# Eighteen of 22 up-projection pairs by Strassen products, and a down stage of its own, in a one-core decoder step

## The chip, the core and the metric

The kernel runs as one program on 1 core of a Trainium2 chip. The metric is the device time of one execution in microseconds (us); of several executions the median is given. The core has five engines: TensorE (PE, matmuls, with weight loads beside them), VectorE (DVE), ScalarE (ACT), GpSimd (POOL) and SyncE (SP), which issues nearly all DMA transfers. Each engine runs its instructions in the order in which the program issued them and waits at an instruction until its operands are there.

## What is computed

One layer of a decoder in float32, for 1,024 prompt tokens and 8 sequences of 4 sample tokens, 1,056 columns in all. The change lies in its last part, the feed-forward network (FFN):

```python
# D_MODEL = 1024, D_FF = 2816
merged = sigmoid(g_M) * (hm @ w_branch_m) + sigmoid(g_A) * (ha @ w_branch_a)
x  = LN1(ALPHA * x + gate1 * (merged @ w_out))
h2 = LN0(x) * (1 + scale2) + shift2
u  = h2 @ w_up + b_up                        # (tokens, 2 * D_FF)
u' = conv_b + sum_j ux[:, j:j+L] * conv_w[j] # causal depthwise convolution, width 3
f  = (gelu(u'_a) * u'_g) @ w_down + b_down   # a: first half of u', g: second half
x  = LN2(ALPHA * x + gate2 * f)
```

In the convolution a prompt token sees the two tokens before it; a sample sequence has two history columns of its own. The last two columns of u of every sequence are outputs too.

## The kernel before, in words

**Numbers and tiles.** Every float32 operand is split into a high part (a cast) and a low part (value minus high part), and each product is three matmuls: high by high, high by low, low by high. Activations lie with features on the 128 partitions and the 1,056 tokens along the free axis, and one such tile of 128 x 1056 float32 (528 KB) fills a slot of a pool of 43 (`slot`, L124; `drop` gives it back). Tokens are worked in three tiles of 384, 384 and 288. `Stream` (L385) carries the weights of direct blocks: `load` issues the DMA of a raw weight part, `prep` makes its high part on ACT (L422) and its low part on DVE (L426), `ahead_of` keeps the next part split and the one after on its way. `group` (L440) makes one output block of 128 rows for one token tile: 8 parts of the contraction by 3 matmuls. Its result lies in one of three PSUM banks used in turn (`lbank`, L146).

**Side work.** The program is one function. Work that is not matmuls is written as generators in a queue, `sides`. `pulse(us)` (L167), called beside each matmul group, advances a planner's clock; for every planned microsecond it takes `rate[0]` steps of the generator at the head (`step_side`, L159). So the rates decide where in each engine's order the side work lands. `later(us, fn)` (L156) puts off one action, mostly a store.

**Strassen pairs.** Ten pairs of blocks of the input projection are made in another way, by the class `Pair` (L1388) and the loop `fast` (L1491). Two output blocks, 1,024 inputs and 1,056 tokens are cut in halves, and seven products of half size (24 matmuls of 264 columns for each of two halves of the tokens) take the place of eight. `tprep` (L1341) makes sums and differences of the activations once; `Pair.step` 0 to 4 makes those of each pair's weights and splits them; `product` (L1451) runs the matmuls in a ring of eight PSUM banks (L1385) and evicts: product 1 by a copy on ACT, products 6, 7 and 5 by an add on DVE (L1465 to L1475), and the results by `put` (L1479), an add of bank, bias and a running sum.

**The FFN before.** The up projection makes 44 direct blocks; block j of the first half and block 22+j of the second form chunk j. ACT evicts u with its bias (L1869, sample tokens apart at L1871). The generator `post` (L1895) does the convolution on DVE, one TENSOR_SCALAR (L1877) and two SCALAR_TENSOR_TENSOR (L1882) over the prompt and three small steps for the samples (L1889 to L1891); then gelu on ACT (L1904) for a first-half block, or the gating multiply (L1908) and the split into `ahi` and `alo` (L337, L338) for a second-half block. Nothing of it leaves the chip's own memory. The down projection is worked in groups of three chunks that are run between up blocks as soon as their chunks are made (`down_group`, L2017): the first group is evicted by ACT into eight accumulators `facc` (L2036), later ones are added by DVE (L2038). After the sixth group `pre` (L1963) scales `facc` by the gate on ACT (L1966), transposes it 128 tokens at a time (PE, banks PD) and adds x1 (L1985), while the last up blocks run. The last group, of four chunks, is made with tokens as output rows (`product`, L2152), and its loop gates, adds, and makes LN2; the last chunk's convolution is done in pieces between (`post_now`).

## Time and profile before

| | |
|---|---|
| median of 3 runs | 1998.91 us (1998.17 to 1999.92) |
| profiled execution, its own time | 1998.65 us |
| its span in the trace | 1996.7 us |
| mean granted TensorE clock | 0.992 |
| matmuls and transposes | 12,837, 1933.1 us busy |
| DVE / ACT / POOL busy | 1114.6 / 737.1 / 301.4 us |
| DMA | 216.03 MB, mean 108 GB/s |

Times in rows of the trace count from the start of the span. In the timeline the first number is an instruction's start, the second its duration, and brackets hold how long its engine stood idle before it and what ended that. Rows of groups give busy time and the mean in ns of one instruction, and behind the second bar the idle time before them. In the table of windows each row is a stretch of time: its length, then the busy time (and count) of PE, weight loads, DVE, ACT and POOL, then granted clock, DMA share and GB/s. The FFN's direct blocks of the whole width begin at about 1245 us of the span, the last stage at about 1930.

### The profile page before, as it was taken

Reading aid. Unit: us, or ns where it says so; the run is one execution under the profiler, and the core shown is the slowest. Engines: PE = TensorE matmul, PEld = TensorE weight load, DVE = VectorE, ACT = ScalarE, POOL = GpSimd, SP = SyncE. Lnnn points to the kernel's source line nnn. Section 1 sums busy time; section 2 is a strip of 40 time slices with the busy share of each in tenths; the row PEclk is TensorE's granted clock in tenths of the full one; section 3 lists DMA queues with packets and bytes.
Section 4 is the critical chain, followed back from the end, with each engine's and each line's share of the span. In section 5 each row is a group of like instructions: output and inputs, shape, how many; then the busy total and the mean of one; then the engine's idle time right before and its main releaser. Section 6 shows DMA issues by size and latency. Waiting matters only on the chain. (4 is left out here: it accounts for less than half of the span.)

```text
span 1996.7 us, 32196 instructions
## 1 busy us (share of the span) xinstructions
PE 1933.1 (97%) x12837; PEld 1834.7 (92%) x12837; DVE 1114.6 (56%) x2374; ACT 737.1 (37%) x1530; POOL 301.4 (15%) x592
## 2 busy tenths in 40 slices
PE   6999999999999999999999999999999999999996
PEld 4999998988899889898889999999999999999995
DVE  5676665556655455563533455574454464546579
ACT  4431234444444554643312355343131312222331
POOL 2000000433441321212000333100000000000007
PEclk9999999999999999999999999999999999999998
DMA  9224342564434103343985141111212020111533
GB/s 296 88 88 157 97 119 79 150 177 134 99 103 127 66 22 121 110 136 107 348 282 166 62 127 55 48 37 46 61 34 62 27 69 27 49 47 48 193 130 129
DMA packets 222942, 216.03 MB, mean 108 GB/s; under 512 B 9745, under 2 KB 199873, under 8 KB 222761
## 3 DMA queue, kind: packets, MB, share of 16 engines
q1 hardware_dynamic: 222013, 213.38, 35.0%
q8 instruction: 100, 1.64, 0.3%
q10 hardware_dynamic: 780, 0.61, 0.1%
q14 instruction: 49, 0.40, 0.1%
HBM read 164.12 MB, written 51.87 MB: 108 GB/s over the span
## 5 line engine op out<-in xcount | busy, mean ns | idle before, releaser
L448 PE MATMUL L<-mhi,whi 128*128 128x384 f32 (+1 forms) x1248 | 408.0, 327 | 4.8 <-DVE r L1824 3.0
L448 PE MATMUL L<-mhi,wlo 128*128 128x384 f32 (+1 forms) x1248 | 403.8, 324 | 1.1 <-DVE wlo L426 1.1
L448 PE MATMUL L<-mlo,whi 128*128 128x384 f32 (+1 forms) x1248 | 404.1, 324 | 0.1
L448 PE MATMUL L<-hhi,whi 128*128 128x384 f32 (+1 forms) x1120 | 370.9, 331 | 0.2
L448 PE MATMUL L<-hlo,whi 128*128 128x384 f32 (+1 forms) x1120 | 362.1, 323 | 0.1
L448 PE MATMUL L<-hhi,wlo 128*128 128x384 f32 (+1 forms) x1120 | 361.7, 323 | 0.0
L426 DVE TENSOR_TENSOR wlo<-wraw,whi 128x1024 fp32r<-128x1024 f32 (+1 forms) x128 | 150.2, 1174 | 305.5 <-ACT whi L422 305.4
L448 PEld LDWEIGHTS L<-mhi,whi 128*128 128x128 f32 x1248 | 235.4, 189 | 6.7 <-DVE r L1824 3.2
L448 PEld LDWEIGHTS L<-mhi,wlo 128*128 128x128 f32 x1248 | 235.1, 188 | 1.7 <-DVE wlo L426 1.7
L448 PEld LDWEIGHTS L<-mlo,whi 128*128 128x128 f32 x1248 | 235.4, 189 | 0.3 <-DVE mlo L1797 0.3
L448 PEld LDWEIGHTS L<-hhi,whi 128*128 128x128 f32 x1120 | 211.2, 189 | 6.9 <-issue 4.8
L448 PEld LDWEIGHTS L<-hlo,whi 128*128 128x128 f32 x1120 | 211.5, 189 | 0.7 <-DVE hlo L1325 0.3
L1869 ACT ACTIVATE u<-L,vT 128x384 f32<-128x384 f32 (+1 forms) x132 | 71.7, 544 | 380.0 <-PE L L448 379.9
L448 PEld LDWEIGHTS L<-hhi,wlo 128*128 128x128 f32 x1120 | 211.1, 188 | 0.0
L422 ACT CAST whi<-wraw 128x1024 fp32r<-128x1024 f32 (+1 forms) x128 | 128.4, 1005 | 32.9 <-DMA wraw<-in_w_up 21.8
L448 PE MATMUL L<-ahi,whi 128*128 128x384 f32 (+1 forms) x432 | 139.7, 323 | 0.0
L448 PE MATMUL L<-ahi,wlo 128*128 128x384 f32 (+1 forms) x432 | 139.5, 323 | 0.0
L448 PE MATMUL L<-alo,whi 128*128 128x384 f32 (+1 forms) x432 | 139.4, 323 | 0.0
L1882 DVE SCALAR_TENSOR_TENSOR y<-u,vT,y 128x1023 f32<-128x1023 f32 (+3 forms) x92 | 113.7, 1236 | 2.5
L1892 POOL COPY ucol<-u 128x2 f32<-128x2 f32 x44 | 10.3, 234 | 631.4 <-ACT u L1869 631.4
L2038 DVE TENSOR_TENSOR facc<-L,facc 128x384 f32<-128x384 f32 (+1 forms) x120 | 62.7, 523 | 58.1 <-PE L L448 58.0
L448 PEld LDWEIGHTS L<-alo,whi 128*128 128x128 f32 x432 | 81.2, 188 | 0.0
(579 smaller groups left out, 3574.8 us busy)
## 6 DMA issues: line engine op xcount, KB each, us to landing
wada<-in_w_ada SPq DMA_DIRECT2D x44, 512.0 KB
wraw<-in_w_up SPq DMA_DIRECT2D x44, 512.0 KB
wraw<-in_w_in SPq DMA_DIRECT2D x32, 512.0 KB
fraw<-in_w_in SPq DMA_DIRECT2D x20, 512.0 KB
wraw<-in_w_down SPq DMA_DIRECT2D x24, 384.0 KB
vD<-fdst SPq DMA_DIRECT2D x8, 528.0 KB
ogD<-fdst SPq DMA_DIRECT2D x8, 528.0 KB
v<-vD SPq DMA_DIRECT2D x8, 528.0 KB
```

The lines of the kernel that those rows point to most:

```text
L422: A.copy(hi[:, :n], t[:, :n])
L426: V.tensor_tensor(lo[:, :n], t[:, :n], hi[:, :n].bitcast(F32), op=OP.subtract)
L448: T.matmul(ps[:, :nt], x[:, c], y[:, t0:t0 + nt], start=i == 0, stop=i == last)
L1869: A.activation(u[:, t0:t0 + n], ps[:, :n], AF.Identity, bias=b)
L1882: V.scalar_tensor_tensor(y[:, f:b], u[:, f - d:b - d], w[i], y[:, f:b], op0=OP.mult, op1=OP.add)
L1892: G.tensor_copy(aux["ucol"][:, c, 0:2], u[:, SEQ - 2:SEQ])
L2038: V.tensor_tensor(fx, ps[:, :nt], fx, op=OP.add)
```

## The change

Four chunks (0 to 3) keep their direct up blocks. The 18 pairs of chunks 4 to 21 go through `fast` as Strassen pairs, with results summed in place in their destination tiles (`inplace`). `first_up_pair`, 23 steps of side work during the last three direct blocks, joins h2's parts again and makes the sums of activations and of the first pair's weights. A convolution's first pass is now ACT's. Every u leaves for DRAM in some form: of the direct chunks u itself (`uD`); of chunks 4 to 10 the finished product of gelu and gate (`aD3`); of chunks 11 to 21 the second block convolved (`yD`) and the first block's u (`uD`).

The down projection then stands alone, in six groups of 3, 4, 4, 4, 3 and 4 chunks: [4, 5, 6], [7, 11, 12, 0], [8, 13, 14, 1], [9, 15, 16, 2], [10, 17, 3], [18, 19, 20, 21]. The generator `chunk` brings each chunk back, does what is left of it and splits it; `operands` takes side steps until a group's chunks are all issued. The fifth group goes through its output blocks once for each token tile (`down_by_tokens`), scales each by the gate and leaves transposes and the add of x1 as delayed steps, so that three of the nine fall behind the group. The rows for the last stage's gate come earlier (`gate_rows2`); `post_now` goes away. The diff, cut to its core:

```diff
+RATE_T, RATE_U, RATE_D, RATE_P = 0.75, 0.7, 0.8, 0.9
-    KG = [3, 3, 3, 3, 3, 3, 4]
+    ND = 4
+    WHOLE = 7
+    ready_, rest = deque(range(ND, ND + WHOLE)), deque(range(ND + WHOLE, 22))
+    KG = [3, 4, 4, 4, 3, 4]
+    chunks_of = [[ready_.popleft() for _ in range(3)]]
+    for i in range(4):
+        chunks_of.append([ready_.popleft(), rest.popleft()] + ([rest.popleft()] if i < 3 else []) + [i])
+    chunks_of.append(list(rest))
...
-    def tprep():
+    def tprep(joined=False):
         for kp in range(4):
+            if joined:
+                for k in (2 * kp, 2 * kp + 1):
+                    hf[k] = slot(name="hf")
+                    hi, lo = opnd["x"][k]
+                    V.tensor_tensor(hf[k], hi.bitcast(F32), lo.bitcast(F32), op=OP.add)
+                yield
...
-            u1, u2, u3, u5 = (u[:, g, :] for u in (U1, U2, U3, U5))
+            if self.inplace:
+                if p in (1, 6) and not g:
+                    self.dst[p // 6] = slot(name="fdst")
+                o = [quarters(self.dst[i])[:, g] if i in self.dst else None for i in range(2)]
...
-            for pos, p in enumerate((1, 3, 6, 2, 7, 4, 5) if n else (1, 3, 2, 6, 7, 4, 5)):
+            for pos, p in enumerate((1, 3, 2, 6, *order_) if not n and swap else (1, 3, 6, 2, *order_)):
...
+    def conv(c, u, y):
...
+        A.activation(y[:, :SEQ], u[:, :SEQ], AF.Identity, bias=b, scale=w[2])
+        A.copy(us[:, :, 2:6], to3(u[:, SEQ:]))
         G.tensor_copy(us[:, :, 0:2], aux["hist"][:, :, :, c])
+        yield
+        V.scalar_tensor_tensor(y[:, 1:SEQ], u[:, :SEQ - 1], w[1], y[:, 1:SEQ], op0=OP.mult, op1=OP.add)
+        yield
+        V.scalar_tensor_tensor(y[:, 2:SEQ], u[:, :SEQ - 2], w[0], y[:, 2:SEQ], op0=OP.mult, op1=OP.add)
+        yield
...
+    def post(c, u):
         y = slot(name="y")
+        yield from conv(c, u, y)
+        drop(u)
+        yield
+        if c >= 22:
+            if c - 22 < ND + WHOLE:
+                ya[c - 22] = y
+            else:
+                to_dram(yD, c, y)
+            return
+        A.activation(y, y, AF.Gelu_apprx_tanh)
+        yield
+        V.tensor_tensor(y, y, ya[c], op=OP.mult)
+        drop(ya.pop(c))
+        to_dram(aD3, c, y)
+        yield
...
+    def chunk(j):
...
+        if j in aD3:
+            y = load(aD3[j])
...
+        else:
+            u = load(uD[j])
+            if 22 + j in yD:
+                y2 = load(yD[22 + j])
...
+            else:
+                u2 = load(uD[22 + j])
...
+                yield from conv(22 + j, u2, y2)
...
+            yield from conv(j, u, y)
...
+            A.activation(y, y, AF.Gelu_apprx_tanh)
+            yield
+            V.tensor_tensor(y, y, y2, op=OP.mult)
+            drop(y2)
+        hi, lo = slot(F32R, "ahi"), slot(F32R, "alo")
+        A.copy(hi, y)
+        yield
+        V.tensor_tensor(lo, y, hi.bitcast(F32), op=OP.subtract)
...
+    def operands(gi):
+        base = sum(KG[:gi])
+        while len(acts2) < base + KG[gi]:
+            step_side()
+        return {k: acts2[base + k] for k in range(KG[gi])}
...
+    def down_by_tokens(gi):
+        a = operands(gi)
+        for ti in range(3):
+            for q in range(4):
...
+                for sub in range(2):
+                    down_block(gi, q, sub, ti, a)
+                    j = 2 * q + sub
+                    f = facc[j][:, t0:t0 + np_]
+                    A.activation(f, f, AF.Copy, scale=modT[:, 5, j, 0:1])
...
+            spread(pre(ti), 1.1)
...
+    def first_up_pair():
+        sums = tprep(True)
+        for i in range(23):
+            if i in (10, 11, 22):
+                upairs[0].step((10, 11, 22).index(i))
+            else:
+                next(sums)
+            yield
...
+    sides.append(first_up_pair())
+    rate[0] = RATE_T
+    for i in range(NF, 2 * ND):
+        if i == NF + 1:
+            upairs[0].load()
...
+    rate[0] = RATE_U
+    chunk_gens = deque(chunk(j) for j in dorder)
...
+    fast(upairs, up_end, (7, 5, 4), lambda n: None)
...
+    for _ in range(3):
+        chunk_gens.popleft()
+    for i in range(11):
+        sides.append(chunk_gens.popleft())
+    sides.append(gate_rows2())
+    sides.extend(chunk_gens)
+    for gi in range(len(KG) - 2):
+        rate[0] = RATE_D
+        down_group(gi)
+    rate[0] = RATE_P
+    down_by_tokens(len(KG) - 2)
```

Line numbers in the following rows are each program's own. The first place is DVE in the up projection. Before, in a direct chunk's second block (`wlo` is a weight's low part, `y` the convolution, `us` the sample columns, `alo` the low part for the down projection):

```order
L426 TENSOR_TENSOR wlo_834_15246<-wraw_830_15154,whi_833_15245 128x1024
L1877 TENSOR_SCALAR y_836_15263<-u_832_15182,vT_88 128x1024
L1882 SCALAR_TENSOR_TENSOR y_836_15263<-u_832_15182,vT_88,y_836_15263 128x1023
L1882 SCALAR_TENSOR_TENSOR y_836_15263<-u_832_15182,vT_88,y_836_15263 128x1022
L1889 TENSOR_SCALAR y_836_15263<-us_15183,vT_88 128x32
L1890 SCALAR_TENSOR_TENSOR y_836_15263<-us_15183,vT_88,y_836_15263 128x32
L1891 SCALAR_TENSOR_TENSOR y_836_15263<-us_15183,vT_88,y_836_15263 128x32
L1908 TENSOR_TENSOR y_831_15171<-y_831_15171,y_836_15263 128x1056
```

And in the change, in an early pair, where `fdst` is a pair's result (L1497 is `put`), and `flo` and `fq` are low parts of the next product's weights:

```order
L1497 SCALAR_TENSOR_TENSOR fdst_734_13349<-L0_71,vT_88,fdst_734_13349 128x264
L1907 SCALAR_TENSOR_TENSOR y_741_13507<-fdst_734_13349,vT_88,y_741_13507 128x1023
L1428 TENSOR_TENSOR flo_744_13529<-fsum_737_13430,fhi_743_13528 128x1024
L1909 SCALAR_TENSOR_TENSOR y_741_13507<-fdst_734_13349,vT_88,y_741_13507 128x1022
L1497 SCALAR_TENSOR_TENSOR fdst_727_13273<-PF_77,vT_88,fdst_727_13273 128x264
L1912 TENSOR_SCALAR y_741_13507<-us_13508,vT_88 128x32
L1913 SCALAR_TENSOR_TENSOR y_741_13507<-us_13508,vT_88,y_741_13507 128x32
L1914 SCALAR_TENSOR_TENSOR y_741_13507<-us_13508,vT_88,y_741_13507 128x32
L1497 SCALAR_TENSOR_TENSOR fdst_727_13273<-PG_78,vT_88,fdst_727_13273 128x264
L1448 TENSOR_TENSOR fq_745_13564<-fraw_736_13366,fq_745_13564 128x512
L1428 TENSOR_TENSOR flo_747_13568<-fsum_738_13431,fhi_746_13567 128x1024
```

A block's convolution steps stand directly behind its last `put`, and ahead of low parts of weights.

The second place is ACT at the end of the first down group. Before:

```order
L2036 ACTIVATE facc_737_13533<-L2_73,vT_88 128x384
L2036 ACTIVATE facc_737_13533<-L0_71,vT_88 128x384
L2036 ACTIVATE facc_737_13533<-L1_72,vT_88 128x288
L422 CAST whi_740_13568<-wraw_735_13492 128x1024
L1869 ACTIVATE u_743_13598<-L2_73,vT_88 128x384
```

In the change (L2101 is the eviction, `ld` a reloaded block; L1903 a convolution's first pass, L1904 its sample copy, L1995 the gelu, L2000 the cast that makes the operand):

```order
L2101 ACTIVATE facc_1011_17557<-L2_73,vT_88 128x384
L2101 ACTIVATE facc_1011_17557<-L0_71,vT_88 128x384
L2101 ACTIVATE facc_1011_17557<-L1_72,vT_88 128x288
L1903 ACTIVATE y_1014_17593<-ld_1013_17577,vT_88 128x1024
L1904 COPY us_17594<-ld_1013_17577 128x8x4
L1903 ACTIVATE y_1015_17605<-ld_1012_17575,vT_88 128x1024
L1904 COPY us_17606<-ld_1012_17575 128x8x4
L1995 ACTIVATE y_1015_17605<-y_1015_17605 128x1056
L2000 CAST ahi_1016_17619<-y_1015_17605 128x1056
```

Both passes, the gelu and the cast of chunk 0 stand behind the group's last eviction; `ahi_1016` is an operand of the second group, which follows on PE with no other work between.

The third place is DVE at the end of the third down group, in the change (L2103 adds into `facc`, L1997 multiplies by the gate, L2002 makes the low part):

```order
L2103 TENSOR_TENSOR facc_1011_17557<-L1_72,facc_1011_17557 128x288
L1907 SCALAR_TENSOR_TENSOR y_1080_18493<-ld_1077_18421,vT_88,y_1080_18493 128x1023
L1909 SCALAR_TENSOR_TENSOR y_1080_18493<-ld_1077_18421,vT_88,y_1080_18493 128x1022
L1912 TENSOR_SCALAR y_1080_18493<-us_18494,vT_88 128x32
L1913 SCALAR_TENSOR_TENSOR y_1080_18493<-us_18494,vT_88,y_1080_18493 128x32
L1914 SCALAR_TENSOR_TENSOR y_1080_18493<-us_18494,vT_88,y_1080_18493 128x32
L1997 TENSOR_TENSOR y_1080_18493<-y_1080_18493,y_1079_18445 128x1056
L2002 TENSOR_TENSOR alo_1082_18508<-y_1080_18493,ahi_1081_18507 128x1056
```

Here one convolution, the multiply and the low part of chunk 2, an operand of the fourth group, stand behind the third group's last add.

## The prediction

> **What bounds the kernel now.** I read the page's busy shares first, then the chain of waits, then the places that the change replaces.

> ```profile
> PE 1933.1 (97%) x12837; PEld 1834.7 (92%) x12837; DVE 1114.6 (56%) x2374; ACT 737.1 (37%) x1530; POOL 301.4 (15%) x592
> ```

> ```profile
> 1262.98 601.22 PE L L448 x3735
> ...
> 1868.33 0.87 PE PD L197 x8
> ```

> TensorE (PE) sets the pace of both FFN stages: in the chain (second fence) it runs 601 us on end, nothing waits in it. So the question is what the change saves on PE, and where VectorE (DVE) or ScalarE (ACT) becomes late. In the timeline, ACT's second eviction of one up block and of the next give the price of a direct block; ACT's first copy of one Strassen pair and of the next give that of a pair in the input projection.

> ```profile
> 1302.70 0.58 ACT L1869 ACTIVATE u<-L,vT 128x384 f32<-128x384 f32 x1 [2.75 <-PE L L448]
> ...
> 1314.26 0.58 ACT L1869 ACTIVATE u<-L,vT 128x384 f32<-128x384 f32 x1 [3.55 <-PE L L448]
> ```

> ```profile
> 183.09 0.38 ACT L1461 COPY hf<-L 128x264 f32<-128x264 f32 x1 [9.33 <-PE L L1457]
> ...
> 203.66 0.38 ACT L1461 COPY hf<-PE 128x264 f32<-128x264 f32 x1 [9.13 <-PE PE L1457]
> ```

> A direct block is 11.56 us (72 matmuls), a pair of blocks 23.12; a Strassen pair is 20.57 us (168 matmuls of 264 columns), so a product (24 matmuls) is 1.47.

> **What the change takes off PE.** 18 pairs x (23.12 - 20.57) = **45.9 us**. Also, three of the nine groups of transposes of the accumulated output (0.87 us each, the row at 1868.33) go behind the first products of the last stage, which DVE paces: **2.6**. In that stage the last block's convolution goes away, but those three tiles' adds come in.

> ```profile
> 1938.70:1960.00 21.30, 21.30 (x97) 17.35 (x96) 20.09 (x34) 5.03 (x7) 12.25 (x17) 1.00 0.21 69
> 1960.00:1980.60 20.60, 20.60 (x91) 14.86 (x90) 20.22 (x27) 4.98 (x4) 18.89 (x17) 1.00 0.44 159
> ```

> ```profile
> 1941.42 0.36 DVE L1877 TENSOR_SCALAR y<-u,vT 128x256 f32<-128x256 f32 x1
> ...
> 1945.19 0.69 DVE L2169 TENSOR_TENSOR L<-L,gp 128x512 f32<-128x512 f32 x1
> ```

> DVE (fourth number) is full; 3.8 us of it leave (1941.42 to 1945.19), and the third product, from which DVE paces, comes 2.6 later: **1.2** won. Gains 49.7 us.

> **What it adds: DVE in the early pairs.** In the input projection a pair leaves DVE 40% idle:

> ```profile
> 180.00:200.00 20.00, 20.00 (x166) 19.92 (x165) 11.87 (x22) 4.22 (x6) 0.00 (x0) 1.00 0.48 159
> ```

> ```profile
> L1416 DVE TENSOR_TENSOR flo<-fsum,fhi 128x1024 fp32r<-128x1024 f32 x20 | 24.5, 1224 | 17.4 <-ACT fhi L1415 17.1
> L1479 DVE SCALAR_TENSOR_TENSOR fdst<-L,vT,hf 128x264 f32<-128x264 f32 x28 | 13.5, 489 | 8.2 <-PE L L1457 8.1
> ...
> L1436 DVE TENSOR_TENSOR fq<-fraw,fq 128x512 fp32r<-128x512 f32 x10 | 6.8, 684 | 0.0
> ...
> L1411 DVE TENSOR_TENSOR fsum<-fraw 128x512 f32<-128x512 f32 x9 | 6.2, 687 | 1.4 <-DMA fraw<-in_w_in 1.3
> ...
> L1467 DVE TENSOR_TENSOR hf<-L,hf 128x264 f32<-128x264 f32 x9 | 3.9, 432 | 7.6 <-PE L L1457 7.6
> ```

> Here the pair also carries the convolution. Groups of DVE and then of ACT from 1245 to 1930 us:

> ```profile
> L1882 DVE SCALAR_TENSOR_TENSOR y<-u,vT,y 128x1023 f32<-128x1023 f32 x43 | 55.1, 1282 | 1.1
> ...
> L426 DVE TENSOR_TENSOR wlo<-wraw,whi 128x1024 fp32r<-128x1024 f32 x43 | 52.5, 1223 | 178.3 <-ACT whi L422 178.3
> L2038 DVE TENSOR_TENSOR facc<-L,facc 128x384 f32<-128x384 f32 x80 | 44.5, 556 | 41.5 <-PE L L448 41.5
> ...
> L1908 DVE TENSOR_TENSOR y<-y,y 128x1056 f32<-128x1056 f32 x21 | 26.4, 1255 | 0.6
> L338 DVE TENSOR_TENSOR alo<-y,ahi 128x1056 fp32r<-128x1056 f32 x21 | 26.4, 1255 | 11.4 <-ACT ahi L337 11.2
> ...
> L1889 DVE TENSOR_SCALAR y<-us,vT 128x32 f32<-128x32 f32 x43 | 12.8, 297 | 0.0
> L1890 DVE SCALAR_TENSOR_TENSOR y<-us,vT,y 128x32 f32<-128x32 f32 x43 | 10.9, 253 | 5.2 <-DVE y L1889 0.9
> ...
> L1985 DVE SCALAR_TENSOR_TENSOR x1r<-x1r,PD 128x512 f32<-128x512 f32 x16 | 10.2, 682 | 2.9 <-DMA x1r<-x1D 1.5 <-PE PD L197 1.2
> ```

> ```profile
> L1904 ACT ACTIVATE y<-y 128x1056 f32<-128x1056 f32 x22 | 23.9, 1088 | 8.6 <-DVE y L1891 8.6
> L337 ACT CAST ahi<-y 128x1056 fp32r<-128x1056 f32 x21 | 22.6, 1078 | 62.3 <-DVE y L1908 62.3
> ...
> L1871 ACT ACTIVATE us<-L,vT 128x32 f32<-128x32 f32 x43 | 12.1, 281 | 0.0
> ...
> L1966 ACT ACTIVATE facc<-facc,modT 128x1024 f32<-128x1024 f32 x8 | 8.7, 1142 | 0.0
> ```

> For the seven pairs whose both blocks are finished in the up stage (chunks 4 to 10): three low parts 3.67, fq 0.68, four sums 2.75, six adds 2.58, eight puts 3.91, four convolution steps 5.13, six small sample steps 1.6, the gating multiply 1.26: 21.6. Successive ones overlap by 0.08 (the first row below is 1.22 long, the next starts after 1.14), so about 19.5.

> ```profile
> 188.45 1.22 DVE L1416 TENSOR_TENSOR flo<-fsum,fhi 128x1024 fp32r<-128x1024 f32 x1
> 189.59 0.43 DVE L1465 TENSOR_TENSOR hf<-PD,hf 128x264 f32<-128x264 f32 x1
> ```

> DVE works in order, and right behind the last put stands a convolution step that needs ACT's pass over the same block (1.14, as L1966): 1.2 idle; the next low part waits for a cast that ACT does behind that pass, 0.7; the multiply waits for the gelu, 0.4. So a cycle is 21.9 against PE's 20.57: 1.4 x 7 = **10 us**. Behind DVE stand the next product's weights, for which PE waits. Lower end 0 (the eight PSUM banks cover it), upper end 24 (no overlap, (21.6 + 2.4 - 20.6) x 7). I take the sum, since both its parts are rows of like work. The other eleven pairs lose one convolution and the multiply: 15 us of DVE, covered, 0.

> **The start of the pairs.** Between the last norm and the first pair, DVE forms 8 joins (1.26), 16 halves and 4 low halves (0.69), 4 low parts (1.26), 4 sums (0.69), 2 pair parts and 2 weight parts (1.22): about 37, less 3 for overlap, plus four casts of 1.1 in line, starting 2.7 into the three direct blocks, since its next weight part waits for the last eviction before them: 41. PE has 3 x 11.56 + 2.94 = 37.6 of cover. PE waits 3.5. The input projection's start shows such a wait, and what comes after:

> ```profile
> 101.48 0.28 PE L1457 MATMUL PD<-hhi,flo 128*128 128x264 f32 x1
> 104.31 0.59 PE L1457 MATMUL PE<-thi,fhi 128*128 128x264 f32 x1 [2.54 <-ACT fhi L1415]
> ...
> 105.71 0.59 PE L1457 MATMUL PE<-thi,flo 128*128 128x264 f32 x1 [0.59 <-DVE flo L1416]
> ...
> 110.50 0.42 PE L1457 MATMUL L<-thi,flo 128*128 128x264 f32 x1
> 110.72 0.35 PE L1457 MATMUL L<-th,fhi 128*128 128x264 f32 x1
> ```

> ```profile
> 105.00:110.00 5.00, 4.41 (x20) 4.29 (x20) 3.53 (x5) 3.63 (x7) 0.00 (x0) 0.50 0.77 215
> ```

> The granted clock is 0.50: matmuls are 0.22 us apart until 110.72, 23 of them, then 0.12. That costs 2.4 us beside the wait. So 3.5 + 2.4 = **5.9** (bounds 0 and 9). [...]

> **The down stage.** Evictions of its first group are ACT's, and the last chunk of the second group (chunk 0, both convolutions still to do) stands on ACT and DVE behind the first group's last eviction; PE's order has the second group right behind the first, and its first block needs that chunk after 9 matmuls (1.6 us). From PE's last matmul: eviction 0.6, pass 1.14, steps 2.55, small steps 0.95, second block's 2.55 and 0.95, gelu 1.1, multiply 1.25, cast 1.1, low part 1.25: 13.4. PE waits 11.8 and has a dip: **14.2**. Before the fourth group chunk 2 has one convolution, gelu, multiply, cast and low part behind the third's last eviction: 0.5 + 2.55 + 0.95 + 1.1 + 1.25 + 1.1 + 1.25 = 8.7, less 1.8: 6.9 + 2.4 = **9.3**. Before the third only a low part stands there: **0.8**. Bounds: if half is hidden, 12; if loads come late too, 34. They are serial chains of known rows, so I take them whole.

> Inside groups two to four DVE has 30 to 41 us in 46.2 (24 adds, two to four convolutions, weights): covered, with **2** for evictions that stand behind a step. The fifth, by token tiles, has 24 adds, three convolutions, three multiplies, four low parts, seven weight parts and twelve adds of x1 (L1985): about 44 after overlap against PE's 34.7 + 5.2: **4** (0 to 8).

> Stores and loads of 37 blocks of 528 KB: in the input projection two loads of 512 KB are there 5 us after issue, and here a pair's sums stand 7 us behind their issue; in the down stage 11 or more slots are free, so that SP issues far ahead. I take 0; the cover gone, each late load costs PE its lateness.

> ```profile
> 188.40 1.54 SPq L1399 DMA_DIRECT2D fraw<-in_w_in  x2
> ```

> ```profile
> 193.48 1.05 ACT L1415 CAST fhi<-fraw 128x1024 fp32r<-128x1024 f32 x1 [6.14 <-DMA fraw<-in_w_in]
> ```

> **Sum.** Costs 10 + 5.9 + 14.2 + 9.3 + 0.8 + 2 + 4 = 46.2; gains 49.7: -3.5. The profiled execution took 1998.65 (span 1996.7), 0.26 below the median: 1998.9 - 3.5 = **1995.4 us**. What can be told from no change is about 0.2%, 4 us.

> **Rivals.** (1) *DVE never comes last in the pairs*: the eight banks absorb the handoffs, and the fifth group drains into the last stage. For it: DVE's sum without waits, 19.5, is below 20.57. Against: a mean of 95% leaves no room for in-order waits. 1995.4 - 10 - 4 = 1981. (2) *DVE's handoffs with ACT decide the down stage too*, slower: each convolved chunk has four (pass, gelu, cast, small copy) of 1.1; three chunks a group make 13 us where 5 to 9 are spare. It decides once less than two thirds of them are covered: 4 us in three groups and 1 more in seven pairs, 1995.4 + 19 = 2014. For it: three PSUM banks (6 us of PE) stand between. Against: the old down groups never let PE wait. (3) *Loads late*: 1.4 us a pair at seven pairs, 2005. [...] That the change doesn't do what it says is excluded: the program's order shows 3,024 matmuls of 264 columns for 2,592 of 384 and 288.

> **How the numbers follow.** Forecast 0.40 (1985 to 2004), (1) 0.27, (2) 0.21, (3) 0.05, (4) 0.07. Faster: 0.12 + 0.27 + 0.06 = 0.45; same 0.24 + 0.02 = 0.26; slower 0.04 + 0.20 + 0.05 = 0.29. The range 1978 to 2012 takes in (1) and most of (2).

> **What would show it.** Right: pairs 5 to 11 at 21.5 to 22.5 us, later ones at 20.6; PE idle some 12 us at the second down group and some 7 at the fourth, each with a granted clock of 0.5 behind it. Wrong: early pairs at 20.6; PE waiting for loads; waits of several us inside groups two to four.

## The result, and the profile after

The changed kernel took **2053.29 us** (median of 4 runs, 2050.92 to 2054.95); beside it the kernel before took 1998.68. The ratio is 1.0271, with a 95% interval of 1.0254 to 1.0289: slower by 2.7%. The forecast was 1995.4 (1978 to 2012). PE is busy for 1916.1 us instead of 1933.1, and waits more:

```profile
PE 1916.1 (93%) x13269; PEld 1807.0 (88%) x13269; DVE 1266.5 (62%) x2688; ACT 783.1 (38%) x1560; POOL 334.7 (16%) x592
```

PE's waits from the first Strassen product of the up stage to the end (what PE stood at, what released it; total, times, longest). In the old kernel the table for 1293 to 1930 us, the same stages but the last, is empty.

```profile
PE L L450 <- ACT ahi L2000: 17.1, 3, 10.6
PE PD L197 <- DVE x1r L2054: 12.9, 4, 6.0
PE PF L1469 <- DVE flo L1428: 6.7, 5, 2.3
PE L L1469 <- DVE flo L1428: 6.3, 4, 3.3
PE L L450 <- DVE fdst L1497: 6.3, 1, 6.3
PE PE L1469 <- DVE flo L1428: 6.1, 4, 2.0
PE PD L1469 <- DVE flo L1428: 5.2, 4, 2.1
PE L L450 <- DVE facc L2103: 4.0, 3, 2.7
```

The first row is the waits at the down groups' boundaries, which the forecast had. The rows with `flo` are the pairs: 24.3 us in 17 waits, one at the start of each pair but the first. `x1r` is the add of x1 that empties the transposes' banks, in the fifth group and in the last stage; the 6.3 us stand between the last pair and the first down group.

The next table goes by stage, from PE's first matmul of each to its last (the last stage to the end of the span). "Own work" is PE's time without waits: 18 times 20.57; 216 and 288 matmuls of a direct group, 34.7 and 46.2 us; in the third group 16 transposes of the gate's rows more (48.1, as in the last kernel below); in the fifth the transposes (5.2); in the last stage the old one's length.

| stage | own work | forecast over it | measured | over it |
|---|---|---|---|---|
| pairs, their start included | 370.3 | 10 + 5.9 | 414.7 | 44.4 |
| from there to the end of the first group | 34.7 | 0 | 45.4 | 10.7 |
| second group | 46.2 | 14.2 | 60.5 | 14.3 |
| third | 48.1 | 0.8 | 50.1 | 2.0 |
| fourth | 46.2 | 9.3 | 55.7 | 9.5 |
| fifth | 39.9 | 4 | 57.5 | 17.6 |
| last stage | 66.65 | -1.2 | 75.8 | 9.2 |

With the 2 us inside groups two to four the forecast had 45.0 us over PE's work, the trace has 107.7. So the second and fourth groups came within 0.2 us of the forecast, and the forecast broke in the pairs (28.5 us), at their end (10.7), in the fifth group (13.6) and in the last stage (10.4).

**An early pair**, that is, one in which the convolutions of a chunk that is finished in the up stage are done. First come two windows of one pair each, an early one and a later one (length, PE, weight loads, DVE, ACT, POOL, clock, DMA share, GB/s), then rows of DVE and of ACT from the early one and the start of the next:

```profile
1370.59:1395.02 24.43, 22.37 (x170) 22.16 (x169) 19.72 (x34) 8.00 (x13) 3.00 (x6) 0.92 0.21 66
...
1534.36:1555.79 21.43, 20.73 (x170) 20.51 (x169) 15.59 (x27) 5.58 (x9) 1.93 (x3) 1.00 0.33 101
```

```profile
1391.56 1.22 DVE L1428 TENSOR_TENSOR flo<-fraw,fhi 128x1024 fp32r<-128x1024 f32 x1
...
1394.89 1.28 DVE L1907 SCALAR_TENSOR_TENSOR y<-fdst,vT,y 128x1023 f32<-128x1023 f32 x1 [1.31 <-ACT y L1903]
1398.70 1.23 DVE L1428 TENSOR_TENSOR flo<-fsum,fhi 128x1024 fp32r<-128x1024 f32 x1 [2.52 <-ACT fhi L1427]
```

```profile
1393.62 1.24 ACT L1903 ACTIVATE y<-fdst,vT 128x1024 f32<-128x1024 f32 x1 [6.93 <-DVE fdst L1497]
...
1395.02 0.38 ACT L1479 COPY fdst<-PD 128x264 f32<-128x264 f32 x1
1397.34 0.38 ACT L1479 COPY fdst<-PD 128x264 f32<-128x264 f32 x1 [1.94 <-PE PD L1469]
1397.61 1.05 ACT L1427 CAST fhi<-fsum 128x1024 fp32r<-128x1024 f32 x1
```

DVE's work in a pair is what was forecast: 19.72 us (the upper window; forecast "about 19.5"). Its idle time is not: 4.7 us, not 2.4. The rows show a ring, in which each engine's lateness makes the next one late and comes back to the first. PE waits 2.06 us for `flo` (ready at 1392.8). So the second half of the pair's first product ends late. ACT, which idles, can't make the next cast until it has copied that half out (1397.34), since the cast stands behind the copy. DVE idles 2.52 us for the cast, and gets that much later to the next pair's `flo`. After that wait PE also loses its clock: the granted clock is 0.50 from 1393.37 to 1396.78, and from 1393.46 matmuls stand 0.22 us apart instead of 0.12. The pairs hold seven such stretches of some 110 matmuls in all, which cost some 11 us.

Later pairs (the lower window has 4.1 us less DVE work) still take 21.1 to 23.1 us.

**The end of the pairs**, on DVE, just before PE's first matmul of the down stage at 1714.64:

```profile
1708.90 2.60 DVE L2002 TENSOR_TENSOR alo<-ld,ahi 128x1056 fp32r<-128x1056 f32 x2
1711.41 0.49 DVE L1497 SCALAR_TENSOR_TENSOR fdst<-L,vT,fdst 128x264 f32<-128x264 f32 x1
1712.80 1.28 DVE L1907 SCALAR_TENSOR_TENSOR y<-fdst,vT,y 128x1023 f32<-128x1023 f32 x1 [0.91 <-ACT y L1903]
1714.00 0.49 DVE L1497 SCALAR_TENSOR_TENSOR fdst<-L,vT,fdst 128x264 f32<-128x264 f32 x1
```

The last two evictions (`fdst<-L`) free the banks that the down stage takes first; its own low parts and a convolution step, which waits for ACT, stand ahead of them. DVE had also come late to this place: it idled 4.3 us for a cast of weights, and ACT made that cast only when a store (`ff<-y`) had landed. A tile goes back to the pool when its store is issued, so its next user waits for the store, here 11.89 us:

```profile
1703.44 0.84 ACT L424 CAST whi<-wraw 128x768 fp32r<-128x768 f32 x1 [11.89 <-DMA ff<-y]
```

```profile
1704.31 0.96 DVE L428 TENSOR_TENSOR wlo<-wraw,whi 128x768 fp32r<-128x768 f32 x1 [4.30 <-ACT whi L424]
```

### The profile page after: what moved, and what is told of

Its sections match the earlier page's. It is cut to its first block, busy times and chain, and to the rows that moved or that the text cites. A ratio compares the mean times of both kernels' runs of the same rounds, so it can differ in the third digit from the quotient of the medians.

```text
span 2053.2 us, 33725 instructions
## 1 busy us (share of the span) xinstructions
PE 1916.1 (93%) x13269; PEld 1807.0 (88%) x13269; DVE 1266.5 (62%) x2688; ACT 783.1 (38%) x1560; POOL 334.7 (16%) x592
## 5 line engine op out<-in xcount | busy, mean ns | idle before, releaser
L428 DVE TENSOR_TENSOR wlo<-wraw,whi 128x1024 fp32r<-128x1024 f32 (+1 forms) x88 | 105.7, 1201 | 109.6 <-ACT whi L424 107.8
L450 PE MATMUL L<-ahi,whi 128*128 128x384 f32 (+1 forms) x432 | 144.9, 335 | 29.9 <-ACT ahi L2000 17.1
L450 PE MATMUL L<-mhi,whi 128*128 128x384 f32 (+1 forms) x384 | 126.7, 330 | 6.1 <-DVE r L1841 4.2
L450 PE MATMUL L<-mhi,wlo 128*128 128x384 f32 (+1 forms) x384 | 124.1, 323 | 1.1 <-DVE wlo L428 1.1
L450 PE MATMUL L<-mlo,whi 128*128 128x384 f32 (+1 forms) x384 | 124.0, 323 | 0.1
L450 PEld LDWEIGHTS L<-ahi,whi 128*128 128x128 f32 x432 | 83.6, 194 | 33.7 <-ACT ahi L2000 18.0
L424 ACT CAST whi<-wraw 128x1024 fp32r<-128x1024 f32 (+1 forms) x88 | 89.9, 1023 | 20.4 <-DMA ff<-y 11.9
L1428 DVE TENSOR_TENSOR flo<-fsum,fhi 128x1024 fp32r<-128x1024 f32 x56 | 68.5, 1223 | 46.9 <-ACT fhi L1427 46.4
L450 PEld LDWEIGHTS L<-ahi,wlo 128*128 128x128 f32 x432 | 83.3, 193 | 1.4 <-DVE wlo L428 1.4
L450 PEld LDWEIGHTS L<-mhi,whi 128*128 128x128 f32 x384 | 72.2, 188 | 8.0 <-DVE r L1841 4.7
L1916 POOL COPY ucol<-us 128x16 f32<-128x16 f32 x44 | 32.0, 727 | 276.6 <-ACT us L1904 214.8
```

The costliest lines, as they stand in the source:

```text
L424: A.copy(hi[:, :n], t[:, :n])
L428: V.tensor_tensor(lo[:, :n], t[:, :n], hi[:, :n].bitcast(F32), op=OP.subtract)
L450: T.matmul(ps[:, :nt], x[:, c], y[:, t0:t0 + nt], start=i == 0, stop=i == last)
L1428: V.tensor_tensor(lo[:, :1024], t[:, :1024], hi[:, :1024].bitcast(F32), op=OP.subtract)
L1916: G.tensor_copy(aux["ucol"][:, c, 2:18].rearrange("p (b j) -> p b j", b=8), us[:, :, 4:6])
```

## The experiments

A value without interval is one run; single runs of one kernel here differ by up to 4.5 us (1995.96 to 2000.43 for the kernel before), so the stages' lengths in the trace decide. The times stand beside 2053.29 us for the changed kernel and 1998.68 for the one before.

### The pairs: order or throughput

**e1_lofirst**: the next pair's first low part ahead of the two sums.

```diff
...
+                if self.inplace:
+                    self.pa = self.parts(self.raw[0], True)
                 self.sum(2, self.s(1), self.q(0, 0), OP.subtract)
                 self.sum(4, self.q(0, 1), self.s(2), OP.subtract)
-                self.pa = self.parts(self.raw[0])
+                if self.inplace:
+                    drop(self.raw[0])
+                else:
+                    self.pa = self.parts(self.raw[0])
```

> The changed kernel, but in the up pairs the low part of the next pair's first weights stands on DVE ahead of the two sums of weights, not behind them (1.38 us earlier). In the changed kernel PE waits for it at each pair's start: 1.8 to 2.1 us in pairs 3 to 8 (each followed by some 3.3 us at half clock, another 1.8), 0.4 to 2.3 later. Theory A, order and hand-over: DVE has the time, the operand only stands too late; then waits fall by up to 1.38, the half clock goes with them, early pairs fall from 24.4 to 21.0-21.8 us, late ones by 0.4 to 1, in all some 25 us, 2053 to 2028 (2022 to 2036). Theory B, throughput: DVE's sum with its waits is longer than PE's, order within it changes nothing: early pairs stay at 24, in all 0 to 6 us won by the late pairs, 2047 to 2053.

2032.15 us. Early pairs fell to about 22.1 (the first of them to 23.4), later ones to 20.3 to 22.0; in all 21 us. This is theory A, though the early pairs stayed 0.3 us over its range.

**e2_castfirst**: in the pair's loop the cast and low part of the second weights ahead of the first product.

```diff
+                if pos == 0 and n and pr is not None and pr.inplace:
+                    pr.step(2)
                 if who is not None:
...
                 if pos == 0:
-                    if n:
+                    if not n:
+                        t1_split([1])
+                    elif not pr.inplace:
                         pr.step(2)
-                    else:
-                        t1_split([1])
```

> The changed kernel, but the cast and the low part of each up pair's second group of weights are issued ahead of the pair's first product, not behind it; so on ACT the cast no longer stands behind the two copies out of that product's banks. In the changed kernel DVE idles 2.5 us per early pair for this cast. Theory A (a ring of hand-overs PE, ACT, DVE, PE): DVE wins these 2.5 us back, PE's wait at the next pair's start falls, early pairs from 24.4 to 21.5-22.5, late pairs as they are: 2053 to 2030-2040. Theory B (DVE's work itself): early pairs stay within 0.5 us of 24.4, 2050 to 2053.

2026.91 us: pairs 3 to 18 at 21.0 to 21.2. DVE's waits in the pairs (total, times, longest), in the changed kernel and here:

```profile
DVE flo L1428 <- ACT fhi L1427: 29.5, 18, 3.3
DVE y L1907 <- ACT y L1903: 22.3, 17, 1.3
DVE fsum L1423 <- DMA fraw<-in_w_up: 9.4, 10, 2.4
```

```profile
DVE y L1909 <- ACT y L1905: 3.1, 17, 0.2
...
DVE flo L1428 <- ACT fhi L1427: 2.9, 1, 2.9
...
DVE fsum L1423 <- DMA fraw<-in_w_up: 1.4, 3, 0.7
```

One step in another place (a cast on ACT and its low part on DVE) took away 26.6 us of DVE's waits for that cast, 19.2 of those for the convolution's first pass, and, without a byte less to move, 8 of 9.4 us of late weights. So nearly all of the late loads in the pairs, rival (3), followed from the ring and were no cause of their own. Later pairs gained too, against my expectation that they would stay: they had the same ring, with less in it.

**e3_noconv**: the convolution of chunks 4 to 10 left out.

```diff
-        y = slot(name="y")
-        yield from conv(c, u, y)
-        drop(u)
-        yield
+        if 4 <= c % 22 < 11:
+            y = u
+        else:
+            y = slot(name="y")
+            yield from conv(c, u, y)
+            drop(u)
+            yield
```

> The changed kernel with the convolution of chunks 4 to 10 left out (14 blocks; u is taken for its convolution, so the output differs). If the convolution in the pairs is what lengthens the early ones (both theories on DVE): early pairs fall from 24.4 to about the late pairs' best, 21.1-21.5; 2053 to 2030. If the pairs were long for a cause that has nothing to do with it (order of the products, or weights that arrive late): they stay above 23.

2031.89 us, early pairs 21.1. The convolution's work is what set the ring going; e2 and the next run, which keep all of it, show that it isn't too much work for DVE.

**e7_both**: e1 and e2 in one.

> Both edits of the pairs in one: the low part of the next pair's first weights ahead of the two sums, and the cast of its second weights ahead of the first product. The second alone took the pairs from 24.4 and 21.1-23.1 to 21.1 us each, the first alone to 22.1 and 20.4-21. Theory A, order alone keeps PE waiting: pairs at 20.6-20.7, that is, PE's own work, with DVE at 95% of the time in early pairs; 2053 to 2016-2020. Rival, what is left (0.5 us a pair) is something else, weights that land late or banks: pairs at 21.0-21.1, 2024 to 2027.

2016.68 us; pairs 3 to 8 at 20.6 to 20.7, the pairs together 378.0 us for 370.3 of own work. PE's waits for `flo` fell from 24.3 to 0.7 us.

**e8_whole**: e7, with all 18 pairs finished in the up stage (so the down stage loads 11 blocks fewer) and a faster pace of side work in the first down group.

```diff
-    WHOLE = 7
+    WHOLE = 18
...
-        chunks_of.append([ready_.popleft(), rest.popleft()] + ([rest.popleft()] if i < 3 else []) + [i])
-    chunks_of.append(list(rest))
+        chunks_of.append([ready_.popleft() for _ in range(3 if i < 3 else 2)] + [i])
+    chunks_of.append(list(ready_))
...
-        rate[0] = RATE_D
+        rate[0] = DOWN_RATES[gi]        # 1.25, 0.8, 0.8, 0.8
```

> Both edits of the pairs, all 18 pairs convolved, gated and multiplied in the up stage (not seven), so that the down stage reloads 11 blocks fewer, and 1.25 steps a planned us in the first down group (0.8 in the others as before). Theory A: with the hand-overs mended DVE's work of a full pair fits in PE's 20.6 us, so pairs 8 to 18 stay at 20.6-21.2 with 3.9 us more DVE work each; the first five down groups fall from 263 us to 225-240, since 47 us of DVE work leave them; in all 1980-1998. Theory B, DVE's throughput: pairs 8 to 18 rise to 22-24, 2000-2020.

**1985.15 us**, one run, 13.6 us under the kernel before in the run beside it. This decides between the theories. A pair of the second half, which now carries both convolutions, gelu and multiply:

```profile
1588.36:1609.02 20.66, 20.66 (x170) 20.52 (x169) 19.58 (x33) 7.80 (x12) 3.54 (x6) 1.00 0.24 78
```

DVE is 95% busy, in its program's order, and PE never waits. Rival (1) was right about what is possible ("DVE's sum without waits, 19.5, is below 20.57"), and the forecast's reason against it ("a mean of 95% leaves no room for in-order waits") is refuted: what mattered was where two steps, each a cast and its low part, stood.

### The down stage

**e4_rates**: side work taken faster in the first four groups.

```diff
-        rate[0] = RATE_D
+        rate[0] = DOWN_RATES[gi]        # 1.35, 0.95, 1.1, 1.0
```

> The changed kernel, with the steps of side work taken faster in the first four down groups (1.35, 0.95, 1.1 and 1.0 for 0.8 a planned us), so that the last chunk of the second group and that of the fourth are issued on DVE and ACT among the evictions of the group before and not behind them. Theory A: the boundaries are serial chains; PE's waits of 10.6 us (with 14.3 us lost in the second group) and of about 9 in the fourth go, 2053 to 2032 (2028 to 2038), and the fifth group loses less too, since more of its chunks are ready. Rival: ACT and DVE then evict too late inside the groups (three banks), which get longer by as much: 2045 to 2055.

2033.88 us. Second group 60.5 to 47.9, fourth 55.7 to 50.3, fifth 57.5 to 49.3: the boundaries were the serial chains of the forecast. The rival took part of it back: the first group grew from 39.0 to 46.6, since its evictions on ACT stand behind steps that wait for DVE:

```profile
1740.28 1.07 ACT L2001 CAST ahi<-y 128x1056 fp32r<-128x1056 f32 x1 [2.20 <-DVE y L1998]
1741.26 1.05 ACT L2102 ACTIVATE facc<-L,vT 128x384 f32<-128x384 f32 x2
```

**e5_prefetch**: x1's tiles for the transposes loaded when their steps are planned.

```diff
-        fetch(ids[0])
+        for i in ids[:3]:
+            fetch(i)
+        return pre_steps(ti, ids, xs_, fetch)
+
+    def pre_steps(ti, ids, xs_, fetch):
+
         for i in ids:
             n, x = rows_of(i), xs_[i]
-            fetch(i + 1)
+            if i + 1 not in xs_:
+                fetch(i + 1)
```

> The changed kernel, with the three tiles of x1 that each step of transposes needs loaded when the step is planned, so that for the last three they are issued ahead of the two gain rows and four tiles (3 MB) of the last stage. In the changed kernel DVE stands 8.8 us in that stage until the first of them lands, PE 6.1. Theory A, a late load behind 3 MB on one queue: DVE's wait falls to 0-2 us, the last stage from 75.8 to 68-70 us, 2053 to 2045-2048. Rival, the DMA engines are full (342 to 385 GB/s there) and something must be late: another tile is, stage 73 or more, 2050 to 2053.

2044.97 us. The last stage took 75.8 us in the changed kernel, where DVE stood 8.78 us for a tile of x1 (first row); here it took 68.6, with 3.3 us of wait for another tile (second):

```profile
1990.10 1.29 DVE L2054 SCALAR_TENSOR_TENSOR x1r<-x1r,PD 128x512 f32<-128x512 f32 x2 [8.78 <-DMA x1r<-x1D]
```

```profile
DVE pre L2289 <- DMA pre<-preD: 3.3, 1, 3.3
```

Both theories had a part in it: the wait moved to another tile, with 5.5 of its 8.8 us gone. The fifth group grew from 57.5 to 60.6 us here, and about 4 of the 8.3 us won in all lie in the pairs, which this edit leaves alone; so what it is worth is read from the last stage.

**e6_spread**: the delayed steps of transposes and adds of x1 in the fifth group 1.9 us apart (`spread(pre(ti), 1.9)` for `spread(pre(ti), 1.1)`).

> The changed kernel, with the steps of transposes and adds of x1 in the fifth group planned 1.9 us apart, not 1.1. In the changed kernel the group takes 57.5 us for 39.9 us of PE's work, and PE waits at transposes for the adds that empty their banks (8.8 us in that group) while these stand behind other work on DVE. Theory A, order: waits at transposes fall to 1-3 us, the group to 50-52, 2053 to 2046-2049 (the rest of the transposes then stands in the last stage). Theory B, DVE's sum in that group is over PE's: the waits move to the evictions, group 55 or more, 2051 to 2055.

2045.62 us. The fifth group fell only to 55.3 (the last stage to 72.7): its waits at transposes for x1 (5.6 us) went, those at evictions rose from 4.0 to 7.3. So the waits moved, as theory B has it; but DVE was busy for 40.3 of those 55.3 us, so its sum wasn't the bound either. What helps is to take the chunks' steps out from between the evictions: 49.3 in e4 (DVE 29.9 busy), 44.7 in e8 (26.8). (With this spacing, and with those of 1.8 and 1.5 for two tiles below, the last steps of one token tile run into the next one's: row tile 6 is transposed into the banks before tile 5 has been added from them, so 128 rows of y differ. The work is the same in number.)

### The end of the pairs

**f1_tail**: e8 with e5's loads and a spacing of 1.8 us for the first two token tiles.

> The last kernel (both edits of the pairs, all 18 pairs finished in the up stage, 1.25 steps in the first down group; 1985.15 us) with the early loads of x1 and the steps of transposes 1.8 us apart for the first two token tiles. If the edits add up: the last stage falls from 76.3 to 68-70, the fifth group from 44.7 to 41-43: 1985 to 1974-1978. Rival, they take from each other (the loads fill the queue inside the fifth group): 1979 or more.

1975.08 us; last stage 68.4 (76.3 in e8) and fifth group 43.2 (44.7): the edits add up.

**f2_pairend**: f1, with no side work beside the last products, and the low parts of the first group's operands among and behind the last evictions.

```diff
         elif pos == 5:
-            for _ in range(3):
-                next(chunk_gens[0], None)
+            rate[0] = 0.0
+            for _ in range(3):
+                next(chunk_gens[0], None)
+            for _ in range(2):
+                next(chunk_gens[1], None)
         elif pos == 6:
             for i in (1, 2):
-                for _ in range(4):
+                for _ in range(2):
                     next(chunk_gens[i], None)
...
     fast(upairs, up_end, (7, 5, 4), lambda n: None)
+    for _ in range(2):
+        next(chunk_gens[2], None)
```

> That kernel, and at the end of the pairs no side work, and the low parts of the first down group's operands issued on DVE among the last products' evictions and behind them, not ahead of the last ones. Before the first down group PE waits 6.3 us in the changed kernel (7.8 in the 1985 us one) for a bank whose eviction stands on DVE behind two low parts and a convolution step that waits for ACT; then the clock is at half. Theory A, order on DVE: the wait falls to 0-2 us and the first group from 42.3 to 36-40: 6 to 11 us won against the run beside it. Rival, the operands are late anyway (loads into slots that stores must leave first): wait stays over 4, 0 to 3 us won.

1972.76 us: PE's wait before the first group fell from 8.0 to 3.9, the first group grew by 1.4. The gain of 2.3 us speaks for the rival, the wait for half of each; the runs g0 and g1 below part them.

**f3_start**: f2, with the sums for the first pair begun 14 us earlier (and its weights loaded one block earlier).

> That kernel, and the sums of activations and of the first pair's weights begin 14 us earlier, during the last token tile of the first five direct blocks, at 0.55 steps a planned us. In the changed kernel PE waits 3.2 us for an eviction behind casts in the first pair, 0.5 to 0.8 three times more, and the first pair takes 21.6 us. Theory A: waits fall to under 1, first two pairs to 20.7-21.2: 3 to 6 us won against the run beside it, 1960 to 1968 in all. Rival: DVE then stands in the way of the last norms and evictions of the first blocks: nothing won, or up to 4 us lost.

1967.31 us (3 rounds; ratio 0.9843, 0.9827 to 0.9860). The wait of 3.2 us in the first pair is gone, the pairs take 373.0 us instead of 380.2.

**g0_end** (f2's edit alone, in the changed kernel) and **g0_slots** (four tiles of activation sums given back two products earlier, alone in the changed kernel; its diff):

```diff
         elif pos == 4:
+            drop(*t3s)
             win.prep(DN)
...
-    drop(*t3s, *(t for kp in range(4) for t in t_ops[kp]))
+    drop(*(t for kp in range(4) for t in t_ops[kp]))
```

> The changed kernel, with the end of the pairs alone mended in its order: no side work beside the last products, and the low parts of the first group's operands among and behind the last evictions on DVE. In the changed kernel PE waits 6.3 us at this place. Theory order: wait falls to 0-2 us, 4 to 6 us won. Theory slots (operands wait until a store has left their tile): wait stays at 4-6, under 2.5 us won.

> The changed kernel, with four tiles of activation sums given back to the pool after the last pair's product 7, two products earlier, and nothing else, so that the first group's operands take tiles that no store is still leaving. Theory slots: the casts no longer wait for stores, wait falls from 6.3 to 2-4 us. Theory order: within 1 us of 6.3.

The wait was 6.3 us and the first group 39.0. With the order mended: 1.8 and **34.8** (2048.69 us). With the tiles given back: 4.0 and 40.2 (2054.48 us, no gain that these runs can tell). So order is the main cause and the pool's tiles a part (in both runs the cast of weights still waited some 11 us for the store). In g0_end the group's 4.3 us over its own work went with the wait; which of the two, the wait or the side work ahead of it, had made them, this run does not part.

**g1_slots**: f3, both mended, spacing 1.5.

> The best kernel so far (1967.3 us) with the steps of the first two token tiles in the fifth group 1.5 us apart (at 1.8 those of one tile ran into the next one's) and the four tiles given back early. There the wait was 4.0 us with the order mended. Theory slots for this remainder: wait 0-1.5, 2.5 to 5 us won (the half clock behind it too), 1962-1965. Otherwise 1966-1968.

1961.03 us, wait 0.7: the tiles were the rest. ACT's wait for the store, ahead of its casts of the operands, fell from 6.5 us in f3 to 2.7. The gain, 6.3 us, is more than was expected.

**g2_turns**: g1, with the direct chunk's steps in turn with those of the finished ones.

```diff
+    def in_turn(a, b):
+        live = [a, b]
+        while live:
+            for g in list(live):
+                if next(g, True):
+                    live.remove(g)
+                else:
+                    yield
...
-    for i in range(11):
-        sides.append(chunk_gens.popleft())
-    sides.append(gate_rows2())
+    for js in chunks_of[1:5]:
+        gens = [chunk_gens.popleft() for _ in js]
+        sides.append(in_turn(gens[-1], one_by_one(gens[:-1])))
+        if js is chunks_of[3]:
+            sides.append(gate_rows2())
```

> That kernel, with the steps of the direct chunk in each of the four groups that have one taken in turn with those of its three (two) finished chunks, so that a step on ACT that needs DVE's last step stands two steps behind it. In the first group ACT's evictions stand 3 us behind a gelu and a cast that wait for DVE. Theory hand-over: first group from 42 to 37-39, 1958-1963 in all. Rival, the group is long because its work for ACT is: 41 or more, no gain.

1954.45 us (5 rounds; ratio 0.9786, 0.9773 to 0.9800). First group 40.5 to 35.0, against 34.7 of own work: the hand-overs between DVE and ACT had made it long.

**h1_best** and **h2_nospread**: g2 with 1.5 us for the first token tile alone, and with the change's own 1.1 us throughout, so that every bank is emptied before it is filled.

> The last kernel (1954.45 us), with the steps of transposes 1.5 us apart for the first token tile alone, so that each bank is emptied before it is filled again. The work is the same; fifth group 43-46, in all 1952-1958, 2.0 to 2.4% under the kernel before. If the spacing was what made the fifth group short, it goes back to 47 or more and the whole to 1958-1962.

> That kernel without any spacing (1.1 us, as in the change). Theory: with the chunks' work gone from it the fifth group is no longer bound by DVE and spacing is worth 0 to 2 us: 1952-1959. Otherwise 1959 or more.

1957.98 us (0.9802, 0.9787 to 0.9816) and **1956.23 us** (0.9792, 0.9776 to 0.9809); fifth group 45.4 and 44.7: wider spacing is worth nothing there any more. The second is the best of the kernels that give the whole of the reference's output, 2.1% (1.9 to 2.2) under the kernel before. Its five groups and last stage, in the table of windows:

```profile
1666.20:1701.20 35.00, 34.98 (x217) 34.88 (x218) 25.10 (x31) 24.84 (x41) 9.34 (x12) 1.00 0.65 223
1701.20:1747.60 46.40, 46.40 (x291) 46.40 (x290) 31.86 (x48) 16.84 (x21) 4.31 (x11) 1.00 0.34 105
1747.60:1795.70 48.10, 48.10 (x305) 47.89 (x305) 31.73 (x47) 13.61 (x17) 1.94 (x5) 1.00 0.28 90
1795.70:1842.10 46.40, 46.40 (x291) 46.40 (x290) 24.64 (x38) 9.84 (x10) 0.00 (x0) 1.00 0.26 84
1842.10:1886.70 44.60, 40.98 (x266) 39.79 (x266) 26.82 (x49) 18.31 (x29) 0.00 (x0) 1.00 0.54 185
1886.70:1956.30 69.60, 55.18 (x249) 42.44 (x247) 53.03 (x80) 11.35 (x12) 40.39 (x37) 0.90 0.53 188
```

The first four run at PE's speed. What is still lost is in the fifth (4.7 us) and at the last stage's start (3).

## Why the prediction was wrong, point by point

- **What the change takes off PE** held. With most waits mended the pairs take 373.1 us in the last kernel, 20.7 a pair, for the forecast's 20.57, and of the gain that was forecast (49.7) the last kernel as a whole shows 42.5 us. One slip of count, which entered no sum: a product is 12 matmuls for each half of the tokens, 24 in all and 2.94 us; the prediction and the description put 24 to one half.
- **The early pairs** is the step that failed first. Forecast "21.9 against PE's 20.57", 10 us; measured 22.6 to 24.6 us for pairs 2 to 9, and pairs 1 to 7 alone 22 us over PE's work. The sum of DVE's work was right, the waits were not: I added three waits that I saw in the program's order (1.2, 0.7, 0.4; with 19.5 they make 21.8, not 21.9) and took them as independent. They close a ring through PE's own lateness, the 2.52 us at 1398.70 among them, and I priced no half clock in the pairs, though I did at the start: it came seven times (granted clock 0.50) and cost some 11 us. The upper bound that the prediction gave, 24 us, was nearer than the sum.
- **The other eleven pairs** were put at "covered, 0". Measured 21.1 to 24.3, some 16 us: pairs 8 and 9 still carry steps of the earlier ones, and the rest have the same ring with less in it, and late weights that came of it.
- **The start** was right in size, 5.9 forecast and 5.5 won by the mend in f3, but not in its path: PE waited 3.2 us not for its operands from DVE but for a bank, whose eviction of u on ACT stood behind two casts that waited 5.72 us for DVE's sums. That the size came out is in part luck.
- **The boundaries** were right in place and chain, and each had half clock behind it (granted 0.50 from 1758.59 to 1772.24 and from 1871.23 to 1878.06): 10.59 us of wait (forecast 11.8) and 14.3 in all (14.2) at the second group, 5.9 (6.9) and 9.5 in all (9.3) at the fourth, and e4 took most of it away. That the sums agree so closely is partly luck: the waits came about 1 us shorter, what followed them as much longer.
- **From the last pair to the first group's end** the forecast had nothing. It read the order at the end of that group, not at its beginning, where two low parts (2.60 us) and a convolution step stand ahead of the last evictions on DVE (g0_end took 4.5 of 6.3 us away), and it did not ask which store still holds the tile that an operand is put into (g0_slots, g1_slots).
- **The fifth group** (4 forecast, 17.6 measured): "about 44 after overlap" for DVE was close (42.2 busy), but PE's wait was taken as the excess of one sum over another. With three banks, and each engine in its program's order, steps that waited for another engine stood between PE and its next bank: of the 17.6 us PE waited 7.7 at transposes (5.6 for DVE's add of x1, 2.1 for ACT's gate) and 4.0 at evictions by DVE.
- **The last stage**: -1.2 forecast, 9.2 measured. That x1's tiles come behind 3 MB on the same queue was in the order of SP, which I read for the chunks and not here; DVE stood 8.78 us for the first of them.
- **Rivals.** (1), 1981, is near the time that the change could have had (1985.15 in e8). (2), slower, had the right mechanism, hand-overs between DVE and ACT, but put most of it into the down stage and only 1 us a pair into the pairs. (3) was real in the last stage, and in the pairs a consequence. (4), put at 0.07, that the clock would not fall at the start, is refuted: it was 0.50 there from 1297.79 to 1301.20, and it fell more often than forecast, six times more in the pairs.

## What to carry to other kernels

When work is moved onto an engine that already serves the critical one, a sum of durations says whether it can fit, and only the order says whether it does: follow each operand that the critical engine waits for back through every instruction that stands ahead of it, and look for rings in which the critical engine's lateness feeds its own wait. An engine at 95% held the pace here once two steps stood elsewhere, and at 73% it didn't before. Read the order at both ends of each stage and on the DMA queue too, and try the order before giving up a change: here the same arithmetic was 2.7% slower and, with steps moved and 11 blocks no longer sent out and back, 2.1% faster.

## What was not expected of the hardware

What told them apart in this trace was where a wait lay. The granted clock changes there only at times that lie whole multiples of 3.41 us apart: in the pairs to half at 1297.79, 1342.16, 1369.47, 1393.37, 1417.26, 1465.05 and 1488.94, and back one such step later (two after the second). Here are the steps around three waits, cut at those times (length, PE, weight loads, DVE, ACT, POOL, then the clock). The first holds the whole wait of 1.84 us, the next two share that of 2.04, the last two that of 2.32:

```profile
1366.06:1369.47 3.41, 1.57 (x13) 1.36 (x12) 3.21 (x5) 0.13 (x1) 0.58 (x1) 1.00 0.00 0
1369.47:1372.88 3.41, 3.41 (x18) 3.41 (x17) 1.28 (x1) 1.49 (x3) 1.35 (x2) 0.50 0.02 5
...
1437.74:1441.15 3.41, 1.60 (x14) 1.39 (x12) 3.34 (x6) 0.00 (x0) 0.58 (x1) 1.00 0.01 4
1441.15:1444.57 3.42, 3.19 (x26) 3.19 (x27) 2.11 (x4) 1.84 (x4) 0.99 (x1) 1.00 0.02 5
...
1680.09:1683.50 3.41, 2.52 (x21) 2.31 (x19) 3.31 (x7) 1.05 (x1) 0.58 (x1) 1.00 0.00 0
1683.50:1686.91 3.41, 1.98 (x16) 1.98 (x17) 2.18 (x4) 1.20 (x2) 0.00 (x0) 1.00 0.00 0
```

Of the steps at full clock in the pairs of the changed kernel, from 1292 to 1700 us, each of the seven in which PE idled 1.84 us or more (up to 2.71) was followed by half clock, and none with 1.81 or less. So a wait of 2 us was followed by half clock here when nearly all of it fell into one step.
